# A hybrid decoder layer on one core: attention outputs moved to the next slot, merge in two parts, another dense order

## The chip, the core and the metric

The kernel runs on one core of a Trainium2 chip. A core has a matrix engine (PE, with weight loads PEld that overlap it), a vector engine (DVE), a scalar engine (ACT), GpSimd (POOL), and a sync engine (SP) that issues most DMAs. Matrix products land in PSUM, which has eight banks here, each holding a tile of 128 x 512 float32. Each engine takes its own instructions in order and waits for the others by semaphores. The metric is device microseconds of one execution, as a median over runs.

## The reference

The program is one decoder layer on 512 tokens plus 16 meta tokens, width 1024, all in float32. After a layer norm one wide projection gives queries, keys and values for attention, the inputs of an RWKV-7 recurrence, and two gates:

```python
proj = h @ w_in[l]
q, k, v, zr, gate_att, gate_rwkv = jnp.split(proj, [c0, c1, c2, c3, c4], axis=-1)
att = lax.map(lambda qkv: swa_one(qkv[0], qkv[1], qkv[2], rel_bias, sinks_l), (q, k, v))
rw = rwkv7_time_mix(zr, shift_mu[l], decay_w0[l], ...)
merged = jax.nn.sigmoid(gate_att) * att + jax.nn.sigmoid(gate_rwkv) * rw
h = layer_norm(ALPHA * h + merged @ w_out[l], ln1_g[l], ln1_b[l])
ff = jnp.square(jax.nn.relu(h @ w_ff1[l])) @ w_ff2[l]
h = layer_norm(ALPHA * h + ff, ln2_g[l], ln2_b[l])
```

`swa_one` is sliding-window attention (window 128, 16 query heads, 2 key heads, a learned sink). `rwkv7_time_mix` steps a 64 x 64 state per head along the tokens, normalizes each head's output, adds a bonus term and multiplies by a second gate `g = sigmoid(gl) @ g2`.

## The kernel before

**Dense work.** Each float32 operand is split into a high and a low part, and a dense product is three matrix products (high x high, low x high, high x low; `three`, L330 to L333). A dense *unit* computes 128 output columns of the big projection for all tokens: 8 steps of three products of 512 columns, or 16 steps of 264 columns where all 528 tokens are needed. A unit's weights are loaded and split (L258 on ACT, L261 on DVE) two units ahead. The two PSUM banks of `dn` take the results in turn; an `evict` function reads each.

**Head pairs and slots.** The 16 heads are handled as 8 pairs. The time to the end of the first half is cut into slots `s` = -1 to 8. In slot `s` the recurrence of pair `s-1` is solved (`solve`: blocks of a triangular inverse, folds, a chain of seven steps over chunks of 64 tokens, outputs, norm), pair `s`'s score matrices are made and inverted (`scan`: the inverse is L764 and L768 on DVE), pair `s+1`'s decays are projected (`project_in`: two low-rank products, sums of squares), and attention of pair `s-1` is computed (`attend`) and merged (`join`). The dense units of slots 1 to 6 are gate_att and gate_rwkv of pair `s-1`, then k and r of pair `s+1`, query of pair `s`, and v of pair `s+1`.

**The order.** PE's order is written out by hand. Each dense step yields a planned length; `weave` (L379) walks through the units, adds these lengths up, and calls each small product once the sum has reached its due time and the units that it needs are done. All products whose due times fall between two dense steps stand in one place. The due times are the first numbers in the lists of `scan`, `solve`, `project_in`, `attend` and `join`:

```python
while units and (t < at_ or not set(need) <= finished):
    t += step()
assert set(need) <= finished
what()
```

The order of the other engines and of the DMA queues is made by a scheduler from the order in which the program issues instructions; `ahead(n)` moves a stretch n places up.

**Banks.** PSUM is shared out as 2 banks `dn` (dense), 2 `pg` (scores, turns, folds, sums), 1 `ch`, 1 `Y` and 2 `pat`. The last two serve the low-rank products (L489, L490), the meta scores `scm`, the head transposes `vp`, the attention scores `sp` (L1122), the transposes of probabilities `pt` (L1160), the attention outputs `av` (L1180) and the gate's product `gp` (L1107).

**Attention of a pair.** `attention_scores` makes four blocks of scores; after the fourth come the softmax steps on ACT and DVE (L1144, L1150). `attention_turn(j, i)` transposes half of the probabilities into a `pat` bank and copies it to SBUF twice: `pall` on ACT (L1165) and a masked `pown` on DVE (L1166), one buffer each. `attention_out(j, i)` multiplies them with the values into `av`; after the second half DVE multiplies by the attention gate `ga` (L1186). `aside_gate_rwkv` computes the rwkv gate's dense unit, then three products `gp` and their multiply into `gg` (L1109), and adds 0.7 to the planned time. `merge` loads the bonus term `bvm` (L1190), adds it to the normalized output `z` (L1196), multiplies by `gg` (L1197), adds `ga` (L1198) and, for the first six pairs, stores the result to DRAM as `md` (L1200).

**Afterwards.** In slot 7 `merged_before` reads the six stored results back; in slot 8 the output projection (`o`, L1273 to L1275) takes the dense part's place; the two feed-forward products follow with no small products between.

Of the kernel before, what the change touches and what calls it, by code (L numbers as in the profile page):

```python
# [11 lines left out]
F32 = mybir.dt.float32  # L12
# [8 lines left out]
P = 128  # L21
# [110 lines left out]
def hybrid_layer_kernel(ctx: ExitStack, tc: tile.TileContext, I: dict, out: bass.AP):  # L132
# [213 lines left out]
    def dense(col, spans, evict, before=None, after=None):  # L346

        if before:
            before()
        hi, lo = weights(col)  # L350
        for t0, n in spans:
            ps = dn.tile([P, 512], F32, name="dps", tag="dn")
            for k in range(KT):
                ks = slice(k * P, (k + 1) * P)
                three(
                    ps[:, :n], hi[:, ks], lo[:, ks], hhi[:, k, t0 : t0 + n],
                    hlo[:, k, t0 : t0 + n], first=(k == 0), last=(k == KT - 1),
                )
# [197 lines left out]
    def rwkv_sums(j):  # L556

        S = SS[j]
        sq = S["sq"]
        dv = rw.tile([P, NCH], F32, name="dv", tag="dv", bufs=4)  # L560
        dvm = rw.tile([48, 2], F32, name="dvm", tag="dvm", bufs=4)
        S["dv"], S["dvm"] = dv, dvm
        pool.memset(dvm, 1.0)
        ss = pg.tile([P, 512], F32, name="ss", tag="g")
        s3 = ss[:, 0 : 9 * 2].rearrange("p (c e) -> p c e", e=2)
        for c in range(NCH):
            t0 = NMETA + c * C
# [425 lines left out]
    A = {}  # L993
# [97 lines left out]
    def aside_gate_rwkv(j):  # L1091

        gw = at.tile([P, P], F32, name="gw", tag="gw")
        gwh = at.tile([P, P], F32R, name="gwh", tag="gwh")
        gwl = at.tile([P, P], F32R, name="gwl", tag="gwl")
        nc.sync.dma_start(gw, I["gate_w2"][j])
        act.copy(gwh, gw)
        dve.tensor_tensor(gwl, gw, gwh.bitcast(F32), op=ALU.subtract)

        def evict(ps, t0, n):  # L1100
            t = gate_tile("gg", "r", j)
            act.activation(t, ps, AF.Tanh, scale=0.5)
            A["gg", j] = t

        yield from dense(COL_GRW + j * P, XT_, evict)
        gp = pat.tile([P, 512], F32, name="gp", tag="a")
        three(gp, gwh, gwl, sghi, sglo)  # L1107
        t = A["gg", j]
        dve.scalar_tensor_tensor(t, t, 1.0, gp, op0=ALU.add, op1=ALU.mult)  # L1109
        yield 0.7  # L1110

    def attention_scores(j, n):
        khi, klo, qs, bias = A["khi"], A["klo"], A["qs", j], A["bias", j]
# [76 lines left out]
        nc.sync.dma_start(t, src)  # L1190
        return t

    def merge(j):

        z, bv = SS[j]["z"], aside(at, SS[j]["bv"], "bvm", ABUF["bv"])
        dve.tensor_tensor(z, z, bv, op=ALU.add)  # L1196
        dve.tensor_tensor(z, z, A["gg", j], op=ALU.mult)  # L1197
        dve.tensor_tensor(z, z, A["ga", j], op=ALU.add)  # L1198
        if j < PAIRS - 2:
            nc.sync.dma_start(md[j], z)  # L1200
        else:
            A["m", j] = z
# [127 lines left out]
    values(1)  # L1330
    marks.append(len(units))
    for j in range(1, PAIRS - 1):
        gate_att(j - 1)
        gate_rwkv(j - 1)
        keys(j + 1)
        reads(j + 1)
        query(j)
        values(j + 1)
        marks.append(len(units))
    j = PAIRS - 1  # L1340
    gate_att(j - 1)
    query(j)
    gate_rwkv(j - 1)
    gate_att(j)
    gate_rwkv(j)
    marks.append(len(units))
# [14 lines left out]
    def scan(j):  # L1361

        need = (f"k{j}", f"r{j}", f"v{j}")
        return [
            (0.0, need, F(rwkv_scores, j, 0)),
            (3.2, (), F(rwkv_meta, j)),
            (3.2, (), F(rwkv_scores, j, 1)),
            (3.2, (), F(rwkv_inverse, j)),
            (5.6, (), F(rwkv_bonus, j)),
            (12.4, (), F(rwkv_turn_scores, j)),  # L1370
            (19.0, (), F(rwkv_turn_keys, j)),
            (16.0, (), F(rwkv_inverse_place, j)),
            (21.4, (), F(rwkv_turn_values, j)),
        ]

    def solve(j):

        return [
            (0.0, (), F(rwkv_blocks, j, 0)),
            (0.0, (), F(rwkv_start, j, 0)),  # L1380
            (1.4, (), F(rwkv_blocks, j, 1)),
            (1.4, (), F(rwkv_start, j, 1)),
            (3.2, (), F(rwkv_blocks, j, 2)),
            (3.2, (), F(rwkv_start, j, 2)),
            (4.6, (), F(rwkv_blocks, j, 3)),
            (6.4, (), F(rwkv_turn_inverse, j)),
            (8.4, (), F(rwkv_fold, j, 0)),
            (10.6, (), F(rwkv_fold, j, 1)),
        ] + [(11.6 + 0.95 * c, (), F(rwkv_chain, j, c)) for c in range(NCH - 1)] + [
            (18.6, (), F(rwkv_outputs, j)),  # L1390
            (24.5, (), F(rwkv_norm, j)),
        ]

    def project_in(j):
        return [
            (0.0, (), F(rwkv_begin, j)),
            (5.6, (), F(rwkv_lora, j, 0)),
            (7.4, (), F(rwkv_lora, j, 1)),
            (20.4, (f"k{j}",), F(rwkv_sums, j)),
        ]  # L1400

    def attend(j, t0=9.2, t1=26.0):
        return [
            (t0, (f"q{j}",), F(attention_scores, j, 0)),
            (t0, (), F(attention_scores, j, 1)),
            (t0 + 2.8, (), F(attention_scores, j, 2)),
            (t0 + 4.4, (), F(attention_scores, j, 3)),
            (t1, (), F(attention_turn, j, 0)),
            (t1 + 2.4, (), F(attention_out, j, 0)),
            (t1 + 2.4, (), F(attention_turn, j, 1)),  # L1410
            (t1 + 4.8, (f"ga{j}",), F(attention_out, j, 1)),
        ]

    def join(j, t2):
        return [(t2, (f"gr{j}",), F(merge, j))]

    with tc.manual_schedule(engines={mybir.EngineType.PE}):
        for s in range(-1, PAIRS + 1):
            if s <= PAIRS:
                units[:] = [u for u in all_units[: marks[s + 1]] if u[0] not in finished]  # L1420
            items = []
            if s > 0:
                items += solve(s - 1)
            if 0 <= s < PAIRS:
                items += scan(s)
            if s == -1:
                items += [
                    (0.0, (), F(rwkv_begin, 0)),
                    (9.0, ("wa",), F(rwkv_lora, 0, 0)),
                    (10.4, (), F(rwkv_lora, 0, 1)),  # L1430
                    (20.0, ("k0",), F(rwkv_sums, 0)),
                ]
            if 0 <= s < PAIRS - 1:
                items += project_in(s + 1)
            if s == 0:
                items += [(18.0, ("av",), F(aside_heads, 0))]
            if s == 4:
                items += [(26.0, (), F(aside_heads, 1))]
            if s in (1, 5):
                items += [(8.6, (), turn_heads)]  # L1440
            if 0 < s < PAIRS - 1:
                items += attend(s - 1) + join(s - 1, 31.5)
            if s == PAIRS - 1:
                items += [(10.0, (), merged_before)]
# [231 lines left out]
```

## Time and profile before

| what | us |
|---|---|
| median of 3 runs (lowest, highest) | 999.57 (995.95, 1003.83) |
| the profiled execution | 997.59 |
| its span, first to last instruction | 995.8 |
| slots 0 and before | 112 |
| slots 1 to 6, about 64 each | 389 |
| slot 7 | 59 |
| slot 8 and the rest (norm, feed-forward, last norm) | 436 |

The time of the profiled execution is 1.8 us above its span. The stretches are read from the busy time by windows, with the first product of each slot (`up`, L811) as its border; they are rounded. A row of the timeline starts with its start in us and its length in us, then engine, line, operation, what is written and read, the shape, and in brackets the idle time of the engine before it with what ended it. A row of waits has the engine and the instruction that waited, what it waited for, the sum in us, the number of times and the longest. "x4" merges four like instructions.

### The profile page before, as it was taken

How to read it: one execution, taken by the hardware profiler on the slowest of the kernel's cores; microseconds unless marked ns; L12 is line 12 of the kernel's file. 1: busy time of each engine (PE TensorE's matmuls, PEld its weight loads, DVE VectorE, ACT ScalarE, POOL GpSimd, SP SyncE). 2: the span in 40 equal slices, each digit the busy share in tenths (PEclk: the TensorE clock that was granted, in tenths of full speed). 3: DMA queues.
4: the chain of work that ended last, by engine and by line, in shares of the span. 5: the costliest groups of instructions: out<-in, count | busy, mean ns of one | idle time of the engine just before them, and what ended most of it. 6: DMA issues, size and time to landing. Idle time of an engine off the chain costs nothing.

```text
span 995.8 us, 19206 instructions
## 1 busy us (share of the span) xinstructions
PE 946.2 (95%) x7533; PEld 790.8 (79%) x7533; DVE 654.3 (66%) x1503; ACT 469.6 (47%) x1238; POOL 43.4 (4%) x108
## 2 busy tenths in 40 slices
PE   4999899999999999999998999899999999999996
PEld 3988788888888887878886677788888888888885
DVE  8577688787887878778867865766433234543437
ACT  6535448465584575745736822843422124442220
POOL 2000000010010000100001000100000000000001
PEclk9999899999999999999999999899999999999999
DMA  7544332433224432233444535133232323323232
GB/s 269 94 126 125 99 81 67 126 76 104 76 50 124 104 112 68 70 109 88 129 124 104 171 106 212 64 106 127 86 106 74 117 86 104 95 95 100 71 105 84
DMA packets 82674, 105.47 MB, mean 106 GB/s; under 512 B 47766, under 2 KB 54664, under 8 KB 82584
## 3 DMA queue, kind: packets, MB, share of 16 engines
q1 hardware_dynamic: 81088, 102.16, 35.1%
q10 hardware_dynamic: 1496, 2.08, 0.6%
q8 instruction: 59, 0.97, 0.4%
q14 instruction: 31, 0.25, 0.1%
HBM read 86.29 MB, written 13.74 MB: 100 GB/s over the span
## 4 chain that ended last, share of the span: by engine, by line
PE 69%; DVE 17%; ACT 8%; issue 2%; DMA 2%; SPq 0%; POOL 0%; DVEq 0%; ACTq 0%; POOLq 0%
PE dps L331 12%; PE dps L332 11%; PE dps L333 11%; PE acc L1486 6%; PE acc L1488 6%; PE acc L1487 6%; DVE wlo L261 2%; ACT Z L744 2%; PE sc L659 2%; PE o L1273 2%; PE av L1180 2%; DVE AX L884 2%; PE o L1275 1%; PE o L1274 1%; DVE Xf L768 1%
## 5 line engine op out<-in xcount | busy, mean ns | idle before, releaser
L261 DVE TENSOR_TENSOR wlo<-wraw,whi 128x512 fp32r<-128x512 f32 x242 | 159.4, 685 | 175.3 <-ACT whi L258 174.9
L258 ACT CAST whi<-wraw 128x512 fp32r<-128x512 f32 x242 | 141.8, 618 | 274.3 <-PE dps L332 135.2
L331 PE MATMUL dps<-hhi,whi 128*128 128x264 f32 (+1 forms) x640 | 219.1, 342 | 3.4 <-DVE ftmp L764 1.4
L332 PE MATMUL dps<-hlo,whi 128*128 128x264 f32 (+1 forms) x640 | 204.9, 320 | 1.4 <-DVE hlo L312 1.4
L333 PE MATMUL dps<-hhi,wlo 128*128 128x264 f32 (+1 forms) x640 | 204.1, 319 | 0.4 <-DVE wlo L261 0.4
L331 PEld LDWEIGHTS dps<-hhi,whi 128*128 128x128 f32 x640 | 121.8, 190 | 17.1 <-issue 3.0
L333 PEld LDWEIGHTS dps<-hhi,wlo 128*128 128x128 f32 x640 | 121.4, 190 | 9.1 <-DVE wlo L261 0.6
L332 PEld LDWEIGHTS dps<-hlo,whi 128*128 128x128 f32 x640 | 121.8, 190 | 6.9 <-DVE hlo L312 2.5
L331 PE MATMUL dps<-h1hi,whi 128*128 128x512 f32 (+1 forms) x264 | 100.1, 380 | 3.8 <-ACT h1f L1536 3.8
L332 PE MATMUL dps<-h1lo,whi 128*128 128x512 f32 (+1 forms) x264 | 100.3, 380 | 0.0
L333 PE MATMUL dps<-h1hi,wlo 128*128 128x512 f32 (+1 forms) x264 | 99.9, 379 | 0.0
L331 PEld LDWEIGHTS dps<-h1hi,whi 128*128 128x128 f32 x264 | 50.4, 191 | 12.9 <-ACT h1f L1536 4.1
L332 PEld LDWEIGHTS dps<-h1lo,whi 128*128 128x128 f32 x264 | 50.4, 191 | 9.3 <-DVE h1lo L1542 0.2
L333 PEld LDWEIGHTS dps<-h1hi,wlo 128*128 128x128 f32 x264 | 50.4, 191 | 9.1
L1486 PE MATMUL acc<-whi,hhi 128*128 128x512 f32 x128 | 50.7, 396 | 0.0
L1488 PE MATMUL acc<-whi,hlo 128*128 128x512 f32 x128 | 50.4, 394 | 0.0
L1487 PE MATMUL acc<-wlo,hhi 128*128 128x512 f32 x128 | 50.0, 391 | 0.0
L1486 PE MATMUL acc<-whi,fhi 128*128 128x512 f32 x112 | 43.6, 389 | 0.0
L1487 PE MATMUL acc<-wlo,fhi 128*128 128x512 f32 x112 | 43.6, 389 | 0.0
L1488 PE MATMUL acc<-whi,flo 128*128 128x512 f32 x112 | 43.6, 389 | 0.0
L897 ACT ACTIVATE Z<-ch,PC 64x64 f32<-64x64 f32 x56 | 17.3, 308 | 45.6 <-DVE Z L895 44.3
L744 ACT COPY Z<-vt 64x64 f32<-64x64 f32 x128 | 26.4, 206 | 9.0 <-PE vt L737 7.6
(292 smaller groups left out, 1721.9 us busy)
## 6 DMA issues: line engine op xcount, KB each, us to landing
wraw<-in_w_ff_dram SPq DMA_DIRECT2D x64, 512.0 KB, 3.6
wraw<-in_w_in_dram SPq DMA_DIRECT2D x52, 512.0 KB, 4.1
wraw<-in_w_out_dram SPq DMA_DIRECT2D x8, 512.0 KB, 3.8
xt<-in_x_dram SPq DMA_DIRECT2D x4, 512.0 KB
Nd<-NT SPq DMA_DIRECT2D x16, 128.0 KB, 3.0
bv<-bv SPq DMA_DIRECT2D x8, 256.0 KB
bvm<-bv SPq DMA_DIRECT2D x8, 256.0 KB, 3.4
qs<-qhi SPq DMA_DIRECT2D x16, 128.0 KB, 4.0
```

What stands on the lines that cost most here:

```text
L258: act.copy(hi[:n, qs], raw[:n, qs])
L261: dve.tensor_tensor(lo[:n, qs], raw[:n, qs], hi[:n, qs].bitcast(F32), op=ALU.subtract)
L331: pe.matmul(ps, whi, xhi, start=first, stop=False)
L332: pe.matmul(ps, whi, xlo, start=False, stop=False)
L333: pe.matmul(ps, wlo, xhi, start=False, stop=last)
L659: pe.matmul(scs[e][:, c * P : (c + 1) * P], BK[ER[e], 4 * i + c, :], AXg[ER[e], e, 4 * i + c], start=True, stop=True,)
L744: act.copy(Z[2 * i + cc][64 * (1 - e) : 64 * (1 - e) + 64, e, :], vt[64 * cc : 64 * cc + 64, i * P + e * HD : i * P + (e + 1) * HD],)
L884: dve.tensor_tensor(AXg[:, e, cs], AXg[:, e, cs], gqs[e].rearrange("p (c k t) -> p c k t", c=4, k=2), op=ALU.add,)
L1180: pe.matmul(av[64 * e : 64 * e + 64, (2 * i + n) * P : (2 * i + n + 1) * P], vs[:, 2 * i + n], ps[:, 2 * n + e, :], start=(d == 0), stop=( ...
L1486: pe.matmul(acc[b], xhi[k][:, bs], hi[:, ws], start=first, stop=False)
L1487: pe.matmul(acc[b], xhi[k][:, bs], lo[:, ws], start=False, stop=False)
L1488: pe.matmul(acc[b], xlo[k][:, bs], hi[:, ws], start=False, stop=last)
```

## The change

In slots 1 to 6 the attention outputs of a pair (two transposes, two outputs) leave the end of the slot and are given due times 0.0, 4.6 and 6.4 of the next slot, beside blocks 0, blocks 3 and the inverse's product. `merge` becomes two functions: `merge_rwkv` (bonus and rwkv gate) stays in the pair's slot, at 25.4, and `merge` (attention part and store) goes to 7.0 of the next slot. The rwkv gate's small product becomes a function of its own, `gate_out`, due at 11.6; the 0.7 of planned time goes. The gate units change places (rwkv first; in slot 7 also against the query). The low-rank products move from 5.6 and 7.4 to 7.4 and 8.6; the sums of squares, the key turns and the outputs all stand at 18.6, the value turns and the norm at 23.2. The bank of the sums of squares `ss` comes from `pat` in place of `pg`. Slot 8's own attention outputs keep their times.

```diff
-        ss = pg.tile([P, 512], F32, name="ss", tag="g")
+        ss = pat.tile([P, 512], F32, name="ss", tag="a")
...
+        A["gw", j] = gwh, gwl
         yield from dense(COL_GRW + j * P, XT_, evict)
+
+    def gate_out(j):
         gp = pat.tile([P, 512], F32, name="gp", tag="a")
-        three(gp, gwh, gwl, sghi, sglo)
+        three(gp, *A["gw", j], sghi, sglo)
         t = A["gg", j]
         dve.scalar_tensor_tensor(t, t, 1.0, gp, op0=ALU.add, op1=ALU.mult)
-        yield 0.7
...
-    def merge(j):
-
+    def merge_rwkv(j):
         z, bv = SS[j]["z"], aside(at, SS[j]["bv"], "bvm", ABUF["bv"])
         dve.tensor_tensor(z, z, bv, op=ALU.add)
         dve.tensor_tensor(z, z, A["gg", j], op=ALU.mult)
+
+    def merge(j):
+
+        z = SS[j]["z"]
         dve.tensor_tensor(z, z, A["ga", j], op=ALU.add)
...
     for j in range(1, PAIRS - 1):
+        gate_rwkv(j - 1)
         gate_att(j - 1)
-        gate_rwkv(j - 1)
...
     j = PAIRS - 1
+    gate_rwkv(j - 1)
+    query(j)
     gate_att(j - 1)
-    query(j)
-    gate_rwkv(j - 1)
...
-            (19.0, (), F(rwkv_turn_keys, j)),
+            (18.6, (), F(rwkv_turn_keys, j)),
             (16.0, (), F(rwkv_inverse_place, j)),
-            (21.4, (), F(rwkv_turn_values, j)),
+            (23.2, (), F(rwkv_turn_values, j)),
...
-            (24.5, (), F(rwkv_norm, j)),
+            (23.2, (), F(rwkv_norm, j)),
...
-            (5.6, (), F(rwkv_lora, j, 0)),
-            (7.4, (), F(rwkv_lora, j, 1)),
-            (20.4, (f"k{j}",), F(rwkv_sums, j)),
+            (7.4, (), F(rwkv_lora, j, 0)),
+            (8.6, (), F(rwkv_lora, j, 1)),
+            (18.6, (f"k{j}",), F(rwkv_sums, j)),
...
+    def attend_out(j, t0, t1, t2):
         return [
-            (t0, (f"q{j}",), F(attention_scores, j, 0)),
...
+            (t0, (), F(attention_turn, j, 0)),
+            (t1, (), F(attention_out, j, 0)),
+            (t1, (), F(attention_turn, j, 1)),
+            (t2, (f"ga{j}",), F(attention_out, j, 1)),
         ]
...
+    def join(j, t0, t1, t2):
+        return [
+            (t0, (f"gr{j}",), F(gate_out, j)), (t1, (), F(merge_rwkv, j)), (t2, (), F(merge, j)),
+        ]
...
             if 0 < s < PAIRS - 1:
-                items += attend(s - 1) + join(s - 1, 31.5)
+                items += attend(s - 1, 9.2) + join(s - 1, 11.6, 25.4, 0)[:2]
+            if 1 < s < PAIRS:
+
+                items += attend_out(s - 2, 0.0, 4.6, 6.4) + join(s - 2, 0, 0, 7.0)[2:]
             if s == PAIRS - 1:
                 items += [(10.0, (), merged_before)]
-                items += attend(s - 1, t1=20.5) + join(s - 1, 26.5)
-                items += attend(s, 16.5)[:4]
+                items += attend(s - 1, 10.0) + attend_out(s - 1, 20.5, 22.9, 25.3)
+                items += join(s - 1, 11.6, 26.5, 26.5)
+                items += attend(s, 16.5)
...
             if s == PAIRS:
-                items += attend(s - 1, t1=1.0)[4:] + join(s - 1, 25.5)
+                items += attend_out(s - 1, 1.0, 3.4, 5.8) + join(s - 1, 0.0, 24.5, 25.5)
```

More of the change, by code (lines that the diff above doesn't have):

```diff
@@ L1396, in project_in, with attend @@
             (0.0, (), F(rwkv_begin, j)),
-            (5.6, (), F(rwkv_lora, j, 0)),
-            (7.4, (), F(rwkv_lora, j, 1)),
-            (20.4, (f"k{j}",), F(rwkv_sums, j)),
-        ]
-    def attend(j, t0=9.2, t1=26.0):
-        return [
-            (t0, (f"q{j}",), F(attention_scores, j, 0)),
[L1405 to L1411, printed above, removed]
-        ]
-    def join(j, t2):
-        return [(t2, (f"gr{j}",), F(merge, j))]
+            (7.4, (), F(rwkv_lora, j, 0)),
+            (8.6, (), F(rwkv_lora, j, 1)),
+            (18.6, (f"k{j}",), F(rwkv_sums, j)),
+        ]
+    def attend(j, t0):
+        return [(t0, (f"q{j}",), F(attention_scores, j, 0))] + [
+            (t0 + t, (), F(attention_scores, j, 1 + i)) for i, t in enumerate((0.0, 2.8, 4.4))
+        ]
+    def attend_out(j, t0, t1, t2):
+        return [
+            (t0, (), F(attention_turn, j, 0)),
+            (t1, (), F(attention_out, j, 0)),
+            (t1, (), F(attention_turn, j, 1)),
+            (t2, (f"ga{j}",), F(attention_out, j, 1)),
+        ]
+    def join(j, t0, t1, t2):
+        return [
+            (t0, (f"gr{j}",), F(gate_out, j)), (t1, (), F(merge_rwkv, j)), (t2, (), F(merge, j)),
+        ]
     with tc.manual_schedule(engines={mybir.EngineType.PE}):
```

## The prediction

> **What bounds the kernel now.** I read the page first, then the busy time by stretches, then the matrix engine's (PE's) waits, then its timeline through single slots.
>
> ```profile
> span 995.8 us, 19206 instructions
> PE 946.2 (95%) x7533; PEld 790.8 (79%) x7533; DVE 654.3 (66%) x1503; ACT 469.6 (47%) x1238; POOL 43.4 (4%) x108
> PE 69%; DVE 17%; ACT 8%; issue 2%; DMA 2%; SPq 0%; POOL 0%; DVEq 0%; ACTq 0%; POOLq 0%
> ```
>
> PE is busy for 95% of the span and carries 69% of the chain that ended last. So a moved product pays only if PE stops waiting at it, or if entering and leaving it gets cheaper. The next fence has one whole slot (s=3), and then three pieces of 4 us from slot 4, which starts at 307.87; the columns are length, PE, PEld, DVE, ACT, POOL, clock, DMA.
>
> ```profile
> 243.80:307.87 64.07, 62.72 (x684) 52.78 (x683) 51.71 (x138) 38.42 (x117) 3.91 (x10) 1.00 0.35 91
> 311.87:315.87 4.00, 4.00 (x118) 2.81 (x116) 2.35 (x6) 1.79 (x8) 0.08 (x1) 1.00 0.30 114
> 331.87:335.87 4.00, 4.00 (x38) 3.27 (x34) 4.00 (x13) 1.69 (x5) 0.00 (x0) 1.00 0.10 13
> 335.87:339.87 4.00, 3.68 (x32) 3.07 (x31) 3.88 (x17) 1.79 (x4) 1.54 (x4) 1.00 0.38 134
> ```
>
> A slot is 64.07 us and PE is idle for only 1.35 of them. DVE has room early in the slot (2.35 of 4 us) and none 24 to 32 us in (4.00, 3.88). What PE waits for by name:
>
> ```profile
> PE av L1180 <- DVE pown L1166: 4.9, 5, 1.0
> PE pt L1160 <- ACT sb L1150: 3.5, 2, 2.0
> PE ch L937 <- ACT Z L897: 2.5, 4, 0.8
> PE dps L331 <- DVE r L406: 0.5, 1, 0.5
> ```
>
> Two of these four rows are the attention outputs that the change moves: 4.9 us for `pown`, and of the 3.5 for `sb` one wait of 1.5 (the other, 2.0, is in the last slot, whose order stays).
>
> **The change, part by part.** Times with two decimals below, as 11.66, are planned dense time, worked out from the units' yields (0.682 for a step of 512 columns, 0.372 for one of 264) and the due times; they give the order, not microseconds.
>
> *The places.* A place is a run of small products between two dense steps. Slots 1 to 6 had 25. Gone are 26.24, 28.97 and 30.83 (attention), 19.05 and 20.54 (`tr`, `ss` join `Y` at 18.72), 21.66 (`vt` joins `yt` at 23.50). But the 0.7 that the rwkv gate's unit added to the count goes too, so products that shared a place part: second fold and first chain step (10.91, now 10.91 and 11.66), `axt` and chain step 1 (12.73, now 12.40 and 12.77), chain step 2 and attention scores (13.84, now 13.52 and 13.89). It is 22 places, not 19.
>
> *What a place costs.* I count from the start of the dense product before it to the second one behind it, less two dense spacings (0.233 us for 512 columns, 0.122 for 264).
>
> ```profile
> 358.26 0.39 PE L333 MATMUL dps<-hhi,wlo 128*128 128x512 f32 x1
> 358.50 0.68 PE L1160 MATMUL pt<-con,sb 128*128 128x128 f32 x4
> 358.94 0.48 PE L331 MATMUL dps<-hhi,whi 128*128 128x512 f32 x1
> 359.25 0.40 PE L332 MATMUL dps<-hlo,whi 128*128 128x512 f32 x1
> ...
> 361.59 0.39 PE L333 MATMUL dps<-hhi,wlo 128*128 128x512 f32 x1
> 361.91 0.44 PE L1180 MATMUL av<-pall,vtok 128*64 128x128 f32 x4
> 363.32 0.44 PE L1180 MATMUL av<-pown,vdif 128*64 128x128 f32 x4 [0.97 <-DVE pown L1166]
> ...
> 364.13 0.66 PE L1160 MATMUL pt<-con,sb 128*128 128x128 f32 x4
> 364.54 0.37 PE L331 MATMUL dps<-hhi,whi 128*128 128x264 f32 x1
> 364.75 0.28 PE L332 MATMUL dps<-hlo,whi 128*128 128x264 f32 x1
> ...
> 366.32 0.28 PE L333 MATMUL dps<-hhi,wlo 128*128 128x264 f32 x1
> 366.53 0.44 PE L1180 MATMUL av<-pall,vtok 128*64 128x128 f32 x4
> ...
> 367.73 0.39 PE L331 MATMUL dps<-hhi,whi 128*128 128x264 f32 x1
> 367.95 0.28 PE L332 MATMUL dps<-hlo,whi 128*128 128x264 f32 x1
> ```
>
> First transposes: 359.25 - 358.26 - 0.47 = 0.52. First outputs with second transposes: 364.75 - 361.59 - 0.36 = 2.80. Last outputs: 367.95 - 366.32 - 0.24 = 1.39. Together 4.71 us a slot. The same middle place in slot 6, where `pown` was ready:
>
> ```profile
> 492.03 0.39 PE L333 MATMUL dps<-hhi,wlo 128*128 128x512 f32 x1
> 492.35 0.44 PE L1180 MATMUL av<-pall,vtok 128*64 128x128 f32 x4
> ...
> 493.38 0.66 PE L1160 MATMUL pt<-con,sb 128*128 128x128 f32 x4
> 493.79 0.37 PE L331 MATMUL dps<-hhi,whi 128*128 128x264 f32 x1
> 493.99 0.28 PE L332 MATMUL dps<-hlo,whi 128*128 128x264 f32 x1
> ```
>
> 493.99 - 492.03 - 0.36 = 1.60. So the wait costs 1.2, not its 0.97. The rows also price going in and out: before the transposes (128*128, like the dense work) 0.24, a dense spacing, and after them 0.31, so 0.08 a place; the outputs (128*64) cost 0.21 - 0.12 = 0.09 in and 0.22 - 0.12 = 0.10 out, so 0.19.
>
> *Attention outputs in the next slot.* At 0.00 the transposes follow the scores: 0.52 less 0.08 = 0.44. At 4.77 outputs and transposes follow `blocks` 3: 1.60. At 6.82 the last outputs follow the inverse's product: 1.39 less 0.10 = 1.29. That is 3.33, saving 1.38 a slot for the products of slots 1 to 5, 6.9 in all; for slot 6's about 1.5 (its wait on `sb`) plus 0.2. **Minus 8.6.** It holds only if the moved copies are on time. Of what they add to the early slot a row is
>
> ```profile
> 427.18 0.68 DVE L1166 TENSOR_TENSOR pown<-pt,con 128x512 f32<-128x512 f32 x1
> ```
>
> and with two of these, the `ga` multiply and the last merge add of the same shape, DVE gets 2.7 us more in the early part. `pown` must wait behind the scores' evictions, but has 4.8 planned (7 real, places included) until `out` 0 asks for it; it had 2.7 planned. The moved banks: `meta` at 3.41 needs the bank of the first transposes, `out` 0 a bank of `meta`'s. I cost both at nothing: DVE's room of 1.65 us in the quoted early piece covers one 0.68 copy; without that cover each is a wait of up to 0.7, 0 to 8 us over six slots.
>
> *Merged and split places.* Three go (`tr`, `ss`, `vt`/`yt`), three appear: each 0.08 to 0.19 by the rows above, so 0 within 2 us. I take 0. The Trainium skill, "TensorEngine Tiling (Array Packing)", Key Properties, says that changing the tiling mode drains the engine. The trace has a gap of that sort, 0.19 around the 128*64 outputs. By that rule fewer places help only where mode changes vanish; if all three places fewer saved 0.19 in six slots, the sum would be 3.4 lower, but `Y` and `ss` keep their 128*64 shape between 128*128 neighbours.
>
> *`ss` in `pat`, `tr` and `vt` apart.* No second taker of the `pg` banks stands directly behind `tr` any more. Before, no wait on them is among the quoted rows: 0.
>
> *The low-rank products, later.* This is where a new wait can come. They use both `pat` banks, ACT frees them, and the attention scores behind want them. Before:
>
> ```profile
> 385.55 0.29 PE L489 MATMUL dps<-zw,lhi 128*128 128x264 f32 x1
> 389.21 0.28 PE L489 MATMUL dps<-za,lhi 128*128 128x264 f32 x1
> 391.18 1.16 PE L879 MATMUL gq<-GR,WT 64*128 64x128 f32 x16
> 393.38 0.28 PE L1122 MATMUL sp<-khi,qs 128*128 128x256 f32 x1
> 386.10 0.85 ACT L491 ACTIVATE tw<-dps,drv 128x264 f32<-128x264 f32 x2
> 387.67 1.26 DVE L496 TENSOR_TENSOR_SCAN L<-con,tw 128x528 f32<-128x528 f32 x1 [0.63 <-ACT tw L494]
> 388.96 0.22 ACT L503 ACTIVATE Pm<-L 128x16 f32<-128x16 f32 x1 [1.32 <-DVE L L496]
> 390.32 0.84 ACT L491 ACTIVATE ta<-dps,drv 128x264 f32<-128x264 f32 x2
> ```
>
> From the second product to the scores it was 4.17 us; now one dense step lies between (0.49 + 0.70 = 1.2). From the first to the second it was 3.66; now 0.49 + two dense steps 1.40 + a fold of about 1.3 = 3.2. Counted from the first product, ACT's exponentials start at +3.41, the second pair of tanh would be ready at about +3.7, and behind the exponentials it starts at +4.77 and frees its first bank at +5.2; the scores ask at +4.4. If ACT keeps this order, the wait is 0.9 a slot in 2, 3, 4, 6. In 1 and 5 the head transposes ask for the bank at once: 1.6. Sum 6.8; if tanh goes first, 0. The margin is 0.3 us, less than one DVE operation in the way of the scan, so I take half: **plus 3.4**.
>
> *Chain and fold.* The first chain step no longer follows the fold directly, so the quoted 2.5 us of waits on `Z` lose most of their cause; but steps 1 and 2 now stand two dense steps apart instead of three. Between -2.5 and +3 (0.5 in six slots): I take **-0.5**, beside the nearer row.
>
> *Dense order.* With `ss` and `vt` gone from between, r's first span has one dense span (24 products, 2.9 us) to be evicted before the next unit asks for its bank. The row for `r` shows one wait of 0.5; 0 to 0.5 a slot, 0 taken. Swapping the gates moves no amount of work.
>
> *Queues.* SP issues `md`'s store a slot later, `bvm`'s load and `gw`'s load earlier.
>
> ```profile
> SPq L1190 <- DVE z L1196: 69.9, 7, 13.9
> ```
>
> SP already stands up to 13.9 us before `bvm`'s load, with weight loads behind it. Weights are asked for two units ahead (2 x 24 products of 0.233: 11 us of dense work), and PE still stays 62.7 busy: 0. In slot 7 `merged_before` reads the last `md` right after its store; its reader is a slot away.
>
> **Sum:** -8.6 + 3.4 - 0.5 = -5.7. The profiled execution took 997.6 us, 1.8 more than its span; it would take 991.9. The median before is 999.6 (996 to 1004), so I predict **994 us**, 0.6% less. A measurement here tells about 1% from no change.
>
> **The rivals.** *All waits go* (ACT takes tanh first): -9 to -12, 989; for it speaks the 0.3 us margin, against it ACT's order now. *The new waits eat it*: both `pat` waits in full, chain +2: about 0, 999; for it speak the +4.4 against +5.2. *Slower*: the moved 2.7 us of DVE work don't fit in its early room and push the score and fold evictions in the full stretch (4.00 of 4), so that PE waits for `pat` banks there: up to 2.7 in six slots, +16, with the lora wait +6.8 and -8.6 gained: 1014. It decides once the early room (about 4 us in the first 20) is taken by waiting that can't be filled; against it speaks that the inverse's small steps, which fill that stretch, can slide. *Every place fewer saves its 0.19 in and out*: 3.4 below the forecast, 990.6; against it stand `Y` and `ss` as said. This is the drain rule of the page named above taken in full.
>
> **The numbers.** Forecast 0.5 (990 to 998), all waits gone 0.15, every place saving 0.05, eaten 0.2, slower 0.1. The range 985 to 1004 leaves out the slower rival and the tail below the second. Faster by over 1% (under 989.6): 0.17; within 1%: 0.73; slower: 0.10.
>
> **What would show it.** Right: no row of `av` on `pown`, slots of about 62.6 us, 22 places; the three attention places near 0.44, 1.60 and 1.29; some wait of `sp` on ACT's `ta`. Wrong: waits of `scm` or `av` on banks at 3.41 and 4.77, chain step 2 waiting over 0.5, or `dps` waiting for evictions in the pure dense stretch after 23.50.

## The result, and the profile after

The changed kernel takes 1002.4 us (median of 20 runs, 998.8 to 1006.6) against 997.0 us for the kernel before (20 runs, 994.0 to 1003.8). The ratio is 1.0051, with a 95% interval of 1.0040 to 1.0062. So it is half a per cent slower, where the forecast was 0.6% faster; the time lies inside the range of 985 to 1004. The profiled execution took 998.9 us, 1.9 more than its span. Its page, in the lines that answer to those of before:

```profile
span 997.0 us, 19195 instructions
PE 942.3 (95%) x7533; PEld 792.6 (79%) x7533; DVE 657.1 (66%) x1503; ACT 470.8 (47%) x1238; POOL 47.6 (5%) x108
PE 74%; DVE 12%; ACT 8%; DMA 2%; issue 2%; POOL 1%; SPq 0%; DVEq 0%; ACTq 0%
```

PE is busy for 3.9 us less (946.2 before), and the span is 1.2 us longer: places became cheaper, and more than that came back as waiting. Busy time by stretches, slot 3 as a whole and then four pieces of slot 4, which starts at 303.43 (length, PE, PEld, DVE, ACT, POOL, clock, DMA):

```profile
239.44:303.43 63.99, 62.15 (x683) 53.05 (x683) 51.86 (x138) 38.43 (x117) 4.30 (x10) 1.00 0.34 91
...
327.43:331.43 4.00, 3.33 (x24) 2.49 (x24) 3.97 (x15) 2.92 (x9) 0.00 (x0) 1.00 0.15 40
331.43:335.43 4.00, 4.00 (x38) 3.53 (x36) 4.00 (x12) 1.62 (x5) 0.00 (x0) 1.00 0.08 26
...
355.43:359.43 4.00, 4.00 (x19) 3.25 (x18) 3.88 (x16) 2.98 (x11) 0.00 (x0) 1.00 0.00 0
359.43:363.43 4.00, 3.70 (x28) 3.36 (x26) 3.37 (x5) 3.83 (x17) 0.12 (x1) 1.00 0.47 143
```

Slot 3 is 63.99 us where it was 64.07. PE stands still in two of these pieces of slot 4: 24 to 28 us in, where DVE is near full (3.97 of 4 us), and 56 to 60 us in, where ACT is (3.83 of 4, DVE 3.37). PE's waits by name:

```profile
PE dps L331 <- DVE qlo L1060: 6.9, 6, 1.2
PE up L811 <- DMA X<-Xr: 5.4, 1, 5.4
...
PE ch L937 <- ACT Z L897: 3.1, 4, 1.4
PE pt L1162 <- ACT sb L1152: 3.1, 1, 3.1
PE sp L1124 <- ACT ta L491: 2.7, 4, 0.7
...
PE vp L1041 <- ACT ta L491: 1.5, 1, 1.5
```

The row of `av` on `pown` (4.9 us) is gone. New are six waits of the dense products for `qlo`, the low part of the query, one in each of slots 1 to 6; four waits of the scores for `ta`; and the head transposes `vp`. The first wait, `up` on the inverse's DMA at the start of slot 1, was shorter before:

```profile
PE up L811 <- DMA X<-Xr: 3.7, 1, 3.7
```

**Where the time went.** I count places as the prediction does, and compare from the first product of slot 1 to the end (the tail: 883.5 us before, 887.2 after):

| term | predicted | measured |
|---|---|---|
| attention outputs, slots 1 to 7 | -8.6 | -11.0 |
| low-rank products, scores, `vp` | +3.4 | +8.7 |
| between dense products | 0 | +9.5 |
| chain, folds, merged places, slots 7 and 8 | -0.5 | -3.5 |
| sum | -5.7 | +3.7 |

"Between dense products" is what the spacings outside the places take beyond 0.233 or 0.122 us each. Of its 9.5 us, 7.9 lie at the six waits for `qlo`, 1.29 to 1.33 us each. The changed kernel, profiled twice, gave tails of 887.2 and 887.6.

Before slot 1 lie 109 to 115 us, and over the seventeen profiles of this study that length follows no edit. The wait of `up` for the inverse's DMA lies there, ahead of the tail: it is 1.3 to 3.7 us in the four profiles built on the kernel before and 4.0 to 5.9 us in the thirteen built on the changed one, and why is not shown. Of the 5.4 us between the medians the tail explains 3.7; the rest is not attributed.

The wait for `qlo` in slot 4, by the timeline:

```profile
359.11 3.25 ACT L744 COPY Z<-vt 64x64 f32<-64x64 f32 x15
362.27 0.62 ACT L590 CAST rkh<-rk 128x512 fp32r<-128x512 f32 x1
362.91 0.60 ACT L1059 ACTIVATE qhi<-dps 128x512 fp32r<-128x512 f32 x1
...
360.80 0.75 DVE L585 SCALAR_TENSOR_TENSOR rk<-r,vc,kp 128x512 f32<-128x512 f32 x1
361.46 0.69 DVE L1197 TENSOR_TENSOR z<-z,bvm 128x512 f32<-128x512 f32 x1
362.19 0.69 DVE L1198 TENSOR_TENSOR z<-z,gg 128x512 f32<-128x512 f32 x1
363.54 0.69 DVE L1060 SCALAR_TENSOR_TENSOR qlo<-dps,qhi 128x512 fp32r<-128x512 f32 x1 [0.66 <-ACT qhi L1059]
...
359.81 0.39 PE L333 MATMUL dps<-hhi,wlo 128*128 128x512 f32 x1
360.04 0.28 PE L331 MATMUL dps<-hhi,whi 128*128 128x264 f32 x1
...
364.28 0.39 PE L331 MATMUL dps<-hhi,whi 128*128 128x264 f32 x1 [1.16 <-DVE qlo L1060]
```

The query's last product starts at 359.81. `qhi` starts only at 362.91, because ACT first makes its sixteen copies of `Z` and casts `rk`. DVE is itself busy until 362.88. Both queues reach the query within 0.1 us of one another, and the 24 products of v's first span cover only part of that time.

### The profile page after: what moved, and what is told of

It reads as the page before. It is cut to its first block, busy times and chain, and to the rows that moved or that the text cites. A ratio compares the mean times of both kernels' runs of the same rounds, so it can differ in the third digit from the quotient of the medians.

```text
span 997.0 us, 19195 instructions
## 1 busy us (share of the span) xinstructions
PE 942.3 (95%) x7533; PEld 792.6 (79%) x7533; DVE 657.1 (66%) x1503; ACT 470.8 (47%) x1238; POOL 47.6 (5%) x108
## 4 chain that ended last, share of the span: by engine, by line
PE 74%; DVE 12%; ACT 8%; DMA 2%; issue 2%; POOL 1%; SPq 0%; DVEq 0%; ACTq 0%
PE dps L331 13%; PE dps L332 11%; PE dps L333 11%; PE acc L1498 6%; PE acc L1500 6%; PE acc L1499 6%; PE sc L659 2%; ACT Z L744 2%; PE o L1278 2%; PE av L1182 1%; PE wp L862 1%; DVE wlo L261 1%; PE ch L937 1%; PE o L1280 1%; PE o L1279 1%
## 5 line engine op out<-in xcount | busy, mean ns | idle before, releaser
L1595 DVE TENSOR_TENSOR rl<-rl 128x512 f32<-128x512 f32 (+1 forms) x35 | 22.6, 645 | 11.2 <-ACT fhi L1594 5.8
```

Of the source, the lines that this page charges most:

```text
L1595: dve.tensor_tensor(r, r, r, op=ALU.mult)
```

## The experiments

Below, "tail" is as above. It comes from one profile of each kernel, the medians and ratios from repeated runs against the kernel before on the same chip. The expectations call DVE VectorE, ACT ScalarE and POOL GpSimd.

**1. Two causes, two edits.** The first theory was that the scores' wait and the `qlo` wait come from two due times and could be removed one by one. The changed kernel ran again beside them.

> The changed kernel unaltered, as a yardstick for the other three beside the kernel before. Theory: two new waits of PE, on the low-rank banks (about 0.9 us a slot, 1.9 to 3.2 in slots 1 and 5) and on the query's eviction (1.2 to 1.3 us a slot), together about 16 us, eat the 11 us that the attention outputs gain: ratio about 1.005. Rival (chance of the execution): the ratio is within 1.000 to 1.002 here.

Measured: 1001.1 us, ratio 1.0050 (1.0029 to 1.0070), tail 887.6.

```diff
-            (7.4, (), F(rwkv_lora, j, 0)),
-            (8.6, (), F(rwkv_lora, j, 1)),
+            (7.4, (), F(rwkv_lora, j, 1)),
+            (8.6, (), F(rwkv_lora, j, 0)),
```

> The changed kernel with the two low-rank products in the other order: the iclr one (ta) at 7.4, the decay one (tw), whose tanh is followed by the scan and the exponentials, at 8.6. PE's work and its places are the same. Theory (ACT's exponentials stand ahead of the second tanh and hold the bank): the waits of sp and vp on ta go, 7 to 9 us less than the changed kernel. Rival (the banks are late because DVE or ACT is full in that stretch): the wait moves to tw and stays, under 2 us less.

Measured: 1000.7 us, ratio 1.0034 (1.0019 to 1.0049), tail 886.6. PE's waits:

```profile
PE dps L331 <- DVE qlo L1060: 7.0, 6, 1.2
PE ch L937 <- ACT Z L897: 6.1, 5, 1.6
...
PE sp L1124 <- DVE Xf L768: 1.3, 1, 1.3
PE sp L1124 <- DVE ftmp L764: 1.2, 1, 1.2
```

The waits on `ta` are gone as meant, but the chain waits 3.0 us longer, and two new waits of the scores stand behind the inverse's steps on DVE. With one wait removed, PE came earlier to work that was not ready.

```diff
-            (23.2, (), F(rwkv_turn_values, j)),
+            (21.4, (), F(rwkv_turn_values, j)),
```

> The changed kernel with the value turns back at 21.4, alone in their place; the norm stays at 23.2. Theory (their sixteen copies stand before the query's eviction on ACT): the wait of dps on qlo goes, 6 to 8 us less than the changed kernel, though there is one place more. Rival (places cost by their number): 1 us more than the changed kernel. Rival (the uncovered dense stretch alone makes the query's bank late): the wait stays at over 1 us a slot and the time within 1 us.

Measured: 1004.2 us, ratio 1.0063 (1.0041 to 1.0085), tail 892.5; the `qlo` wait is 7.9 us instead of 6.9, and the median is 3 us above the changed kernel's (the intervals of the ratios overlap), which no side had expected. So the value turns' due time alone is not the cause of the wait. Both edits together:

> Both edits together. Theory: the two waits are independent, 13 to 17 us less than the changed kernel and 8 to 11 less than the kernel before (ratio to it about 0.990). Rival (one hides behind the other): no more than the larger of the two gains.

Measured: 998.9 us, ratio 1.0026 (1.0011 to 1.0041), tail 889.1. The median is 2 us under the changed kernel's, with a longer tail, and the intervals of the two ratios overlap. The theory of two independent waits fell.

**2. Two full stretches.** The second theory: waits move because DVE is full 16 to 32 us into a slot and ACT 40 to 60 us into it. To take DVE work out of the way, the inverse was issued later, with the low-rank halves swapped:

```diff
-            (3.2, (), F(rwkv_inverse, j)),
+            (9.4, (), F(rwkv_inverse, j)),
```

> The changed kernel with its two low-rank halves in the other order and, beside that, the first steps of the inverse due at 9.4 us of a slot in place of 3.2. In the run with the two halves swapped alone, slots 3 and 4 lost the 0.94 us wait of the scores on ScalarE's `ta`, and the second step of the chain then waited 0.94 us for `Z`, whose VectorE work stood behind that engine's full stretch from 16 to 32 us. Theory A (the wait is VectorE's, and goes wherever the fixed order of that engine's work puts it): with the inverse's VectorE steps behind the other work the chain's wait falls under 0.3 us a slot, the tail from slot 1 on is some 2 to 3 us under the 886.6 of the swap alone, and the median is near 997 to 998. Rival (VectorE is full in that stretch whatever its order, so the wait moves again): the scores, the chain or the transposes of the inverse wait as much as before, tail 886 to 889, median 1000 to 1001.

Measured: 1000.0 us, ratio 1.0029 (1.0015 to 1.0042), tail 886.9; the chain's waits on `Z` rose to 7.5 us. The rival holds. For ACT:

```diff
-        for u in range(8):
-            act.activation(s8[:, u], s8[:, u], AF.Copy, scale=sm[:, u : u + 1])
+        pool.tensor_tensor(s8, s8, B64(sm, P), op=ALU.mult)
```

> The changed kernel with the eight scalings of each softmax (ScalarE, some 0.3 us each, 2.4 us a block) done by one multiply on GpSimd. Theory B (the 1.16 us a slot that the dense products wait for VectorE's `qlo` is ScalarE's backlog in its full stretch from 40 to 60 us, since `qhi` stands behind softmax and the copies of `Z`): the wait `dps` on `qlo`, 6.9 us in all, falls under 2, and the tail from slot 1 on falls by 5 to 7 us, from 887.4 to about 881, median near 995. Rival (the wait belongs to the query's own eviction, which nothing covers since the attention outputs left that stretch): `qhi` comes no earlier, the wait stays at 6 to 7 us, the median stays at 1001 or rises if the multiply on GpSimd slows VectorE.

Measured: 1015.3 us, ratio 1.0183 (1.0155 to 1.0211), tail 900.2. The `qlo` wait nearly doubled, to 12.7 us. The timeline of slot 4, which starts at 311.70 in this run:

```profile
363.65 3.47 ACT L744 COPY Z<-vt 64x64 f32<-64x64 f32 x16
371.49 0.62 ACT L590 CAST rkh<-rk 128x512 fp32r<-128x512 f32 x1 [4.37 <-DVE rk L585]
...
365.29 1.88 DVE L547 SCALAR_TENSOR_TENSOR BKm<-u,drv,iP 64x16 f32<-64x16 f32 x1
...
370.71 0.75 DVE L585 SCALAR_TENSOR_TENSOR rk<-r,vc,kp 128x512 f32<-128x512 f32 x1
...
364.79 2.34 POOL L1151 TENSOR_TENSOR sb<-sb,sm 128x1024 f32<-128x1024 f32 x1 [4.65 <-DVE sm L1150]
```

ACT's own backlog is not the whole of the wait: ACT now stands idle for 4.37 us and the wait grew. What ACT waits for is `rk`, from DVE; `qhi` stands behind `rkh` on ACT, and `qlo` behind `rk` on DVE. But the run does not price ACT's part, because DVE lost time to GpSimd as well: an operation of 64 x 16 elements, 0.23 us in the changed kernel, took 1.88 and ended with GpSimd's multiply, and `rk` starts 59.01 us into the slot in place of 57.37. The Trainium skill, "SBUF — State Buffer", section "SBUF: two separate sides", says that VectorE and GpSimd share a pair of ports which one instruction holds to its end; this row agrees.

> Both edits: the low-rank halves swapped with the inverse due at 9.4 us, and the softmax scaling on GpSimd. If the two stretches are apart from one another (VectorE's from 16 to 32 us, ScalarE's from 40 to 60), the gains add: tail 878 to 880, median 991 to 993, under the kernel before. If one backlog only hands its wait to the next place, the result is that of the better one alone, 995 to 1000.

Measured: 1011.1 us, ratio 1.0147 (1.0116 to 1.0177), tail 895.9. Nothing added up, and the time is over both sides' ranges.

> The kernel before with the softmax scaling on GpSimd, as the control. There the attention outputs' places of small products stand between the query's dense products and the next dense ones, and cover ScalarE's backlog. Theory B: nothing waits on that backlog, so the time stays within 1.5 us of the kernel before. Rival (the scaling is on the path anyhow, whatever the places): it gains as much as in the changed kernel, 5 us or more.

Measured: 1003.0 us, ratio 1.0059 (1.0037 to 1.0081), tail 890.7. That is 5.4 us more than the kernel before, so neither side had the time. Slots 2 to 4 stayed within 0.15 us of before, as theory B had it; 6.4 us are lost from slot 8 on, where PE waits 5.3 us for GpSimd's multiply (2.0 for ACT's scaling before), and where the granted clock of PE was 0.50 for 13.7 us from 566.7 (for 3.4 us from 566.0 before):

```profile
PE pt L1159 <- POOL sb L1149: 7.7, 2, 5.3
PE av L1179 <- DVE pown L1165: 5.1, 6, 1.0
```

**3. Parts of the change alone.** First the kernel before with the attention outputs moved and the merge split, and nothing else but the gates' order:

```diff
-                items += attend(s - 1) + join(s - 1, 31.5)
+                items += attend(s - 1)[:4] + join(s - 1, 31.5)[:1]
+            if 1 < s < PAIRS:
+                items += attend_out(s - 2, 0.0, 4.6, 6.4) + join(s - 2, 7.0)[1:]
```

> The kernel before with the attention outputs alone moved (to 0, 4.6 and 6.4 us of the next slot, merge at 7.0 there, its first half at 31.5 in its own slot, the gates in the order that this needs); low-rank work, sums, turns and norm stay as before. Theory (two prices, each with its own cause): the attention outputs get cheaper by some 11 us over the kernel, as in the changed kernel; the dense products wait for `qlo` 1 to 1.3 us a slot, 6 to 8 us in all, since the places that stood behind the query are gone whatever else is changed; the scores do not wait for `ta`, since the low-rank halves keep their places: tail from slot 1 on 3 to 5 us under the 883.5 of before, median near 993. Rival (the `qlo` wait comes from the later turns, sums and merge of the changed kernel): no `qlo` wait over 1 us in all, tail near 873, median 985 to 988.

Measured: 1011.1 us, ratio 1.0121 (1.0082 to 1.0160), tail 897.5.

```profile
PE dps L331 <- DVE qlo L1060: 5.7, 7, 1.4
PE gp L331 <- DVE pown L1166: 4.8, 6, 1.0
PE dps L489 <- DVE gg L1109: 4.6, 6, 0.8
```

The `qlo` wait comes with the move alone, as the theory had it. What neither side expected are the next two rows: the moved transposes now share the `pat` banks with the gate's product, which waits for `pown`, and the low-rank products wait behind that. So the rest of the change (the gate's product apart, the low-rank products later) mends something. The other half:

```diff
-                items += attend(s - 1, 9.2) + join(s - 1, 11.6, 25.4, 0)[:2]
-            if 1 < s < PAIRS:
-
-                items += attend_out(s - 2, 0.0, 4.6, 6.4) + join(s - 2, 0, 0, 7.0)[2:]
+                items += attend(s - 1, 9.2) + attend_out(s - 1, 26.0, 28.4, 30.8)
+                items += join(s - 1, 11.6, 25.4, 31.5)
```

> The changed kernel with the attention outputs back at 26.0, 28.4 and 30.8 us of their own slot and the last part of the merge behind them at 31.5; all else stays changed. Theory: no `qlo` wait (under 1 us in all), the attention places cost what they cost before, with the wait of `av` on `pown` back at some 5 us; the waits of the scores on `ta` and of the chain on `Z` stay at 5 to 9 us, so the tail is 3 to 8 us over the 883.5 of before, 887 to 891, median 1000 to 1004. Rival (the waits of the first half came with the attention outputs that were moved there): they go, and the tail is that of before or 2 us under it, median 995 to 997.

Measured: 1019.0 us, ratio 1.0207 (1.0177 to 1.0237), tail 904.5, far outside both.

```profile
PE av L1182 <- ACT pall L1167: 12.0, 6, 2.0
...
PE sp L1124 <- ACT ta L491: 4.7, 4, 2.4
```

No `qlo` wait is left, as expected. But the wait of `av` did not come back at 5 us for `pown`; it is 12.0 for ACT's `pall`. In slot 4 of this run ACT makes fifteen of the sixteen copies of `Z` from 370.95 to 374.20 and starts `pall` at 374.23, and the outputs start at 374.87. So the product that takes the query's place in that stretch waits too, behind the same copies. Next, the query's dense unit ahead of the reads':

```diff
-        reads(j + 1)
         query(j)
+        reads(j + 1)
```

> The changed kernel with the query's dense products ahead of those of the next pair's reads, so that the query's evictions come ahead of `rk`, `rkh` and the products of the reads on VectorE and ScalarE. In the run with the scaling on GpSimd, ScalarE stood idle 4.4 us ahead of `rkh` and `qhi` and the `qlo` wait still doubled: VectorE's queue (51.3 to 61.8 us of the slot without a gap) holds `rk`, ScalarE's `rkh` waits for it, and `qhi` stands behind `rkh`. Theory (a queue behind `rk` on two engines at once): with the query first its wait falls under 2 us of 6.9, unless the reads' own eviction takes the same place: some wait of the dense products on the reads' `r` (L406) of up to 0.5 us a slot, tail 881 to 885, median 995 to 998. Rival (too little time for both engines in that stretch whatever the order): the dense products wait as long as before, on `r` or `k` in place of `qlo`, or at the start of the next slot on what needs the reads, tail 886 to 890.

Measured: 1004.4 us, ratio 1.0074 (1.0048 to 1.0099), tail 894.5.

```profile
PE dps L331 <- DVE r L406: 10.2, 7, 1.6
```

The wait passed to the reads, and grew: the rival, though its tail of 886 to 890 was too low. The fault is the stretch, not the unit that meets it.

**4. Less work in the stretch.** The sixteen copies of `Z` (64 x 64 elements, 0.207 us each) become four of 64 x 256, into one tile:

```diff
-            for i in range(4):
-                for cc in range(2):
-                    for e in range(2):
-                        act.copy(
-                            Z[2 * i + cc][64 * (1 - e) : 64 * (1 - e) + 64, e, :],
-                            vt[64 * cc : 64 * cc + 64, i * P + e * HD : i * P + (e + 1) * HD],
-                        )
+            v4 = vt.rearrange("p (i e h) -> p i e h", i=4, e=2)
+            for cc in range(2):
+                for e in range(2):
+                    act.copy(Zt[ER[1 - e], cc::2, e, :], v4[ER[cc], :, e, :])
```

> The changed kernel with less in the stretch ahead of `qlo` on both engines: ScalarE's sixteen copies of `Z` made as four of four blocks each (16 x 0.21 us against 4 x about 0.37, from the copies of `tr` of that size: 1.9 us a slot less), and the first half of the merge, two VectorE operations of 0.7 us, moved to 0.0 us of the next slot. Theory (both engines' queues reach `qlo` within 0.1 us of one another in the changed kernel: VectorE is free at 59.47 us of the slot and `qhi` starts at 59.50): `rk` ends 58.1, `rkh` 58.7, `qhi` 59.4, `qlo` 60.1 in place of 60.8, so the wait falls from 1.16 to some 0.4 us a slot, 6.9 to 2 to 3 in all, tail 882 to 884, median 996 to 998. Rival (one engine's queue alone): it falls to under 0.5 us in all, or stays over 5.

Measured: 994.5 us, ratio 0.9962 (0.9940 to 0.9983), tail 882.2.

```profile
PE dps L331 <- DVE qlo L1057: 2.9, 6, 0.5
```

Wait and tail came as expected, the median 1.5 us under its range, but for a part of the reason only. The second edit, the merge's first half issued a slot later, left DVE's written order as it was (in slot 4 of both traces the same 138 operations in the same order), so the gain belongs to the copies. `qlo` then follows the merge on DVE without a gap (the merge's last operation ends at 366.49 us, `qlo` starts at 366.47): DVE has become the last to arrive. Whether that is load or order was the next question. With one 0.69 us product ahead of `rk` left out:

```diff
-            dve.tensor_tensor(AXg[R, e, :, 1, :], rx[R], S["Px"][R, :, 1:], op=ALU.mult)
+            if e == 0:
+                dve.tensor_tensor(AXg[R, e, :, 1, :], rx[R], S["Px"][R, :, 1:], op=ALU.mult)
+            else:
+                act.copy(AXg[R, e, :, 1, :], rx[R])
```

> The changed kernel with the wide copies, and with one of the two products of the reads with `Px` (VectorE, 0.69 us, ahead of `rk`) left out, a copy on ScalarE in its place; its values are not the reference's. The written order of VectorE then has `rkl` and one `wlo` (0.7 us each) ahead of `qlo`, which stood behind it. Theory order (an engine's freed time is filled with the next work of its fixed order, so the wait follows the order, not the load): `rk` ends 57.5 us into slot 3 in place of 58.2, the merge 58.8, `rkl` and `wlo` 60.2, `qlo` ends near 60.9 in place of 60.2, and the wait rises from 0.5 to about 1.1 us a slot, 5 to 7 us in all. Theory load (VectorE was the last limit, and 0.69 us less of it ends the wait): under 0.5 us in all.

Measured: 996.6 us, ratio 0.9990 (0.9968 to 1.0012), tail 882.7.

```profile
PE dps L331 <- DVE qlo L1060: 4.7, 6, 0.8
```

With less work on DVE the wait grew, from 0.5 to 0.8 us a slot (1.1 expected): the written order puts `rkl` and a weight split ahead of `qlo`, and `qhi` is ready 0.5 us before `qlo` starts (362.95 and 363.48 us in slot 4). So at this point the order decides, not the load. Both gains together:

> The changed kernel with the wide copies of `Z` (four in place of sixteen) and the two low-rank halves in the other order. If the two waits are apart from one another: the `qlo` wait at 2 to 3.5 us in all as with the wide copies, the scores' wait on `ta` gone, the chain's wait on `Z` up to 5 to 6 us as in the swap alone, the tail from slot 1 on 1 us under that of the wide copies (882.2), 881 to 882, median 992.5 to 994.5. Rival (the swap's slots run sooner and meet the same full stretch earlier): `qlo` waits 4 us or more again, tail 882 to 884, median 994 to 996.

Measured: 993.5 us, ratio 0.9954 (0.9933 to 0.9975), tail 881.0. The tail is 1.2 us under that of the wide copies, as the swap alone was 1.0 under the changed kernel, so they add as far as one profile each can tell; the ratios' intervals overlap. The chain's waits are 5.5 us, near the swap's 6.1.

**5. The control that decided it.** The kernel before with the same four copies:

> The kernel before with the wide copies of `Z`, the control. There the attention outputs' products stand between the query and the dense products behind it, and nothing waits for `qlo`; what waits is `av` on `pown`, 4.9 us in all, VectorE's, behind the same stretch of ScalarE. Theory (ScalarE's load in that stretch is only on the path where no other place covers it): the time stays within 1.5 us of the kernel before, and the changed kernel with wide copies is the better one by 2 to 4 us. Rival (ScalarE's load holds up VectorE's `pown` too): the wait of `av` falls by 2 us or more and the kernel before gains as much as the changed one, 4 us or more, median 992 to 994.

Measured: 984.1 us, ratio 0.9858 (0.9832 to 0.9884), tail 873.2. The theory fell and the rival holds, beyond the gain it named: the kernel before gains 10.4 us in the tail, the changed one 5. This is the best version measured, 10 us under the changed kernel with the same copies. Why, in two timelines: slot 4 of the kernel before,

```profile
353.63 3.48 ACT L744 COPY Z<-vt 64x64 f32<-64x64 f32 x16 [0.38 <-PE vt L737]
...
357.44 0.48 ACT L412 ACTIVATE r<-dps,drv 128x264 f32<-128x264 f32 x1
...
357.95 0.22 DVE L406 SCALAR_TENSOR_TENSOR r<-edge,vc,r 128x1 f32<-128x1 f32 x1 [1.84 <-ACT r L412]
...
362.58 0.68 DVE L1166 TENSOR_TENSOR pown<-pt,con 128x512 f32<-128x512 f32 x1
```

and slot 3 with the four copies:

```profile
282.75 1.50 ACT L744 COPY Z<-vt 64x256 f32<-64x256 f32 x4 [0.44 <-PE vt L737]
...
284.58 0.48 ACT L412 ACTIVATE r<-dps,drv 128x264 f32<-128x264 f32 x1
...
285.09 0.22 DVE L406 SCALAR_TENSOR_TENSOR r<-edge,vc,r 128x1 f32<-128x1 f32 x1
...
290.07 0.68 DVE L1163 TENSOR_TENSOR pown<-pt,con 128x512 f32<-128x512 f32 x1
```

In the kernel before DVE stands idle here for 1.84 us (1.29 to 1.85 in each of slots 1 to 6), because the reads' eviction on ACT is queued behind the sixteen copies; everything behind it on DVE comes that much later, `pown` among it, and `av` waits 0.97. With four copies the eviction is there in time, the gap is gone, and `av` waits for nothing: the three attention places cost 0.43, 1.61 and 1.22, or 3.26 us, with their outputs where they always stood. In DVE's waits the row for this eviction was, before,

```profile
DVE r L406 <- ACT r L412: 12.2, 7, 1.9
```

and is 1.7 us, once and ahead of slot 1, with the four copies. Another written order does not explain it: in slot 4 of the two traces ACT's order differs by one cast of weights, and DVE's by one operation of 0.18 us (`BKm`), which now comes behind the eviction. With the copies grouped, the move of the outputs has little left to gain, 3.26 against 3.03 us a slot, while its prices stay. A slot is 62.62 us long (64.07 before, 63.99 changed):

```profile
236.94:299.56 62.62, 62.25 (x683) 52.89 (x682) 51.88 (x138) 36.66 (x105) 3.92 (x10) 1.00 0.36 93
```

## Why the prediction was wrong

**The attention outputs: right in mechanism, too small.** The three places came out at 0.39, 1.42 and 1.22 us, 3.03 where 3.33 was predicted. Slot 6's products saved 2.5 us where 1.7 was taken. The term measured -11.0 instead of -8.6.

**What the wait was.** The step read "`av` on `pown`, 4.9 us" as a price of where the outputs stand. It was the end of a chain: ACT's small copies, then the reads' eviction, then DVE's queue, then `pown`. The prediction quoted `pown` as the releaser and did not follow its engine back to its own idle time, though DVE's 12.2 us for `r` stood in the trace. So the move cured a symptom, and the copies took hold of the next product, the dense one behind the query. In the changed kernel they stand behind the reads' eviction (DVE's row for `r` falls from 12.2 us to 1.7, once) and ahead of `rkh` and `qhi`; with four in place of sixteen the `qlo` wait fell from 6.9 to 2.9 us.

**The dense order, 0 taken: the step that failed.** The text costed 0 to 0.5 us a slot for `r` and said that swapping the gates moves no amount of work. The term measured +9.5. Without it the sum would have been -5.8, against -5.7 predicted, but that is luck: the attention outputs and the chain came out 5.4 us better than written and the low-rank products 5.3 us worse. The text did not ask what the places that leave had been covering: of the 4.71 us of attention a slot, 4.2 (the 2.80 and the 1.39 of the prediction's rows) stood between the query's last product and the next use of its bank. Without them PE asks for that bank after v's first span alone, 24 products or 2.9 us, and both ACT and DVE are late. The runs show it from both sides: the move alone brings the wait (5.7 us), and without the move none is left. The list of what would show it wrong named this wait.

**The low-rank wait, taken at half: the second failure.** The working said that ACT would start the second pair of tanh at +4.77 us and the scores would ask at +4.4, and that they would wait 0.9 us a slot. In slot 4:

```profile
323.20 0.29 PE L489 MATMUL dps<-zw,lhi 128*128 128x264 f32 x1
...
328.40 0.38 PE L1124 MATMUL sp<-khi,qs 128*128 128x256 f32 x1 [0.67 <-ACT ta L491]
...
327.87 0.84 ACT L491 ACTIVATE ta<-dps,drv 128x264 f32<-128x264 f32 x2
```

Tanh came at +4.67, the scores at +5.20, the place cost 0.94 us more. In full the term was 6.8; it measured 8.7: 0.9 in each of slots 2, 3, 4 and 6 as worked out, 1.8 in slot 1, and 3.1 in slot 5, where the granted clock of PE was 0.50 for 3.4 us from 393.0. ACT kept its order, and a margin of 0.3 us was no reason to halve a term whose order the trace showed.

**The chain and merged places: near.** Chain, folds and the products beside them got 0.75 us cheaper in slot 3, with no wait at step 2; -0.5 for the whole was too little. In slots 1, 5 and 6 step 2 did wait, 0.46, 0.64 and 0.60 us, of which the last two pass the 0.5 that the prediction named as a sign of being wrong. Merging `Y`, `tr`, `ss` and `vt`, `yt` saved 0.12 us a slot, which fits the 0 taken; 0.19 for each place gone, the drain rule of the Trainium skill's "TensorEngine Tiling (Array Packing)", Key Properties, taken in full, is not what these rows show. There are 22 places, as counted.

**Banks at 3.41 and 4.77, and the full stretch.** No wait of `scm` or `av` on a bank appeared. The slower rival looked for DVE's overload 24 to 32 us in; the larger one lay 52 to 60 us in, on two engines. Nearest to the outcome was "the new waits eat it" (999, one chance in five), with `qlo` in the place of chain step 2. The wait of slot 1's first product was in no term; it lies ahead of the tail.

## What to carry to other kernels

Before moving a product away from a wait, follow the releaser's engine back to its own last idle time, and across engines, until a busy engine without a gap is found, and try the cure there first. Then ask what the product that leaves has been covering: a matrix engine that comes sooner finds the same late eviction at the next bank. Many small operations in one stretch of an in-order engine that is half idle over the span can set the pace. Here grouping them, four copies in place of sixteen, gave 1.4%, more than any rearrangement tried, and the change on top of the grouping costs 10 us.

## What was not expected of the hardware

ACT's copies from PSUM of 64 x 64 elements take 0.207 us and those of 64 x 256 take 0.367: by these two, 0.154 us of each is fixed, and 0.053 goes with 64 columns. The Trainium skill, "Perfetto Trace Analysis", section "Optimizing Scalar/DVE Operations", names such an overhead, with a smaller figure for ScalarE on PSUM (about 51 ns busy, and about twice that as the profile shows an instruction), and advises grouping where an engine is saturated. Here ACT was 47% busy over the span and the grouping paid all the same, because one stretch of it was full (15.19 of 16 us from 343.87 in the kernel before).

A multiply of 128 x 1024 on POOL held up an operation of 64 x 16 on DVE for 1.65 us (1.88 us against 0.23), as shown above.
